# Layer 1's input weights asked for ahead of x, and the value's weights split ahead of the key's copy

## The chip, the cores and the metric

One core of one Trainium2 chip. The metric is the device time of one execution in microseconds (us), lower is better; before the change the median of three runs is 1089.43 us.

## The reference

Two layers of a diffusion backbone over 256 latent and 256 context tokens of 1024 features, float32. Each layer runs attention heads and a gated linear recurrence side by side on one input projection, then a mixture of 16 experts:

```python
def hybrid_layer(x, xc, mod, mod_c, p, router_w, router_b, cos, sin, last):
    ...
    h = modulate(rms_norm(x, p["norm1_g"]), sh1, sc1)
    hc = modulate(rms_norm(xc, p["norm1_g"]), csh1, csc1)
    mix, mix_c = parallel_mixers(h, hc, p, cos, sin, last)
    x = x + g1 * (mix @ p["w_out"])
    h2 = modulate(rms_norm(x, p["norm2_g"]), sh2, sc2)
    ...
    y = grouped_moe(tokens, *moe_w)
    x = x + g2 * y[:B * S].reshape(B, S, D)
```

`parallel_mixers` starts with `q, k, v, u, gb = jnp.split(h @ p["w_in"], cuts, axis=-1)`: the columns of `w_in` are query, key, value, the recurrence's input u and its gate. Layer 1 (the last) needs the context only for keys, values and the recurrence's start.

## The kernel before, in words

The stream x is `xtok`, four tiles of 128 tokens (tiles 0 and 1 context, 2 and 3 latent). In layer 0's experts (`experts`, L1476) each expert gathers its tokens, computes them on TensorE, and POOL adds its results to x in DRAM with a scattering DMA (`scatter`, L1493, into `yd`). x thus lies in DRAM when layer 0 ends. The experts have fixed slots; tokens beyond these are taken by an overflow block (L1759) that is skipped when there are none, as in these runs. Each engine that skips it raises its semaphore counts by what the block would have added: POOL does so for the eight counts of its own DMAs (DMASW0 to DMASW7), with one instruction.

Layer 1 begins in `mixer` (L478). `back_x` (L473) reloads x from `yd`, four DMAs of one tile each on SP's queue; `load_win` (L197) loads `w_in` in four pieces, the first `win_kv` (256 columns, key and value), the second u's 512 columns (`wu` in the code, tile `win`), then query and gate. After the first two come `load_adab` (small loads on POOL's queue) and `load_bd`. `norm1` (L404) then squares each tile of x on ScalarE (L412), forms the scale on VectorE, transposes and scales x on TensorE (`pxt`, with a diagonal matrix `dg`; nine warming products come ahead of it, on tile 1 of x), and shifts the result into `hT` (L427 on VectorE, L429 on ScalarE).

The key's projection (`proj`, `pproj<-hT,win_kv`) multiplies in full float32. All others (`proj3`) use split operands: a rounded part (fp32r) and the rest, three products with 24 matmuls. `piece` (L502) makes the two parts of four chunks of weights, a cast on ScalarE (L508) and a subtraction on VectorE (L509), into one of four slots of `wps`; h is split in the same way into `hh` (L867) and `hl` (L868). The value's two pieces are `pv_`; `k_squares` (L601 on) copies the key from PSUM and squares it, `k_sums` adds the squares up with a matmul (`pks`), for the key's norm.

In layer 1 the order of VectorE, POOL, ScalarE and SP is taken as the code writes it within a `manual_schedule` block, which ended after `norm1`; behind it, and for TensorE in all of this part, a scheduler sets the order.

Of the kernel before, what the change touches and what calls it, by code (L numbers as in the profile page):

```python
# [20 lines left out]
P = 128  # L21
# [91 lines left out]
def backbone(ctx: ExitStack, tc: tile.TileContext, a: dict):  # L113
    nc = tc.nc
    pe, act, dve, pool = nc.tensor, nc.scalar, nc.vector, nc.gpsimd

    def mm(out, lhsT, rhs, start, stop):
        pe.matmul(out, lhsT, rhs, start=start, stop=stop)  # L118
# [10 lines left out]
    def psb(name, tag, n=512):  # L129
        t = pp["pool"].tile([P, 512], F32, name=name, tag=tag, bufs=pp["bufs"][tag])  # L130
        return t[:, 0:n]

    def ps_mm(name, n=512):
        return psb(name, "mm", n)
# [28 lines left out]
    def C(n):  # L163
        o, w = COFF[n]
        return cst[:, o:o + w]
# [8 lines left out]
    def wchunk(name, pl=None, dt=F32):  # L174
        if pl is None:
            pl = wpool
        else:
            return pl.tile([P, 4096], dt, name=name, tag="w")
        if wx["pool"] is not None:
            if wx["only"] is None:  # L180
                i = wx["i"] % wx["n"]
                pl = wpool if i < 4 else wx["first"] if i < 4 + wx["nf"] else wx["pool"]
                wx["i"] += 1
            else:
                pl = wx["only"]
        return pl.tile([P, 4096], dt, name=name, tag="w")
# [10 lines left out]
    def load_win(l, lo, n, t=None):  # L197
        src = a["w_in"][l].rearrange("(k p) n -> p k n", p=P)
        t = (wchunk(f"win{l}_{lo}") if t is None else t)[:, 0:KC * n].rearrange("p (k n) -> p k n", k=KC)
        nc.sync.dma_start(t, src[:, :, lo:lo + n])  # L200
        return t

    WIN = ((512, 256), (768, 512), (0, 512), (1280, 512))
# [102 lines left out]
    def load_adab(l, tmp):  # L306
        for g in (1, 2, 3):
            b = adab[l, g] = tmp.tile([P, 512], F32, name=f"adab{g}", tag=f"adab{g}", bufs=1)
            pool.memset(b[:], 0.0)
            for r in range(2):  # L310
                if g < 3:
                    nc.gpsimd.dma_start(b[r::32, :], a["ada_b"][l, g * 2048:(g + 1) * 2048].rearrange("(j n) -> j n", j=4))
                else:
                    nc.gpsimd.dma_start(b[r:r + 64:32, :], a["norm2_g"][l].rearrange("(j n) -> j n", j=2))
# [158 lines left out]
    def back_x():  # L473

        for t in range(4):
            nc.sync.dma_start(xtok[:, t, :], tokens(yd[0])[t])

    def mixer(l, R, hp, hT, mo):  # L478
# [9 lines left out]
        order = ExitStack()  # L488
        if l:
            order.enter_context(tc.manual_schedule(engines={mybir.EngineType.DVE, mybir.EngineType.Pool, mybir.EngineType.Activation, mybir.EngineType.SP}))  # L490
        kv = tmp.tile([P, 2048], F32, name="win_kv", tag="rec", bufs=1)
        if l:
            back_x()
        win = [load_win(l, *WIN[0], kv), load_win(l, *WIN[1])]
        load_adab(l, tmp)
        if l == 0:
            load_consts()
# [4 lines left out]
        def piece(wv, on):  # L502

            wh, wl = wps[:, 0, wpi[0] % 4], wps[:, 1, wpi[0] % 4]
            wpi[0] += 1
            if len(wv.shape) == 3:
                wh, wl = (v.rearrange("p (k m) -> p k m", k=4) for v in (wh, wl))
            on(wh, wv)  # L508
            dve.tensor_tensor(wl, wv, wh.bitcast(F32), op=OP.subtract)  # L509
            return wh, wl  # L510

        def pieces(w, lo, on=act.copy):
            return [piece(w[:, k0:k0 + 4, lo:lo + P], on) for k0 in (0, 4)]

        if l == 0:
            pv_ = pieces(win[0], P)
        norm1(l, hT, tmp, lp, win[0])
        order.close()
        win += [load_win(l, *w) for w in WIN[2:]]
        if l:  # L520
            pv_ = pieces(win[0], P)
        hh, hl = lp.tile([P, KC, T], F32R, name="hh"), []


# [38 lines left out]
        wkv, wu, wq, wgb = win  # L563
# [7 lines left out]
        def proj3(ws):  # L571

            ps = ps_mm("pproj")
            for k0, (wh, wl) in zip((0, 4), ws):
                for i, (w, h) in enumerate(((wh, hh), (wl, hh), (wh, hl))):
                    for k in range(k0, k0 + 4):
                        mm(ps, w[:, k - k0, :], h[:, k, :] if h is hh else h[k // 2][:, k % 2, :], k + i == 0, k + i == KC + 1)
            return ps
# [22 lines left out]
        def k_squares(ps):  # L601
            act.copy(kT[:], ps)
            sq = t2("sqk")
            act.activation(sq[:], kT[:], AF.Square)
            return sq

        def k_sums(sq):
            pks = psb("pks", "sc")
            mm(pks, C("blk"), sq[:], True, True)
            return pks  # L610
# [252 lines left out]
        for k in range(KC):  # L863
            if k % 2 == 0:
                hl.append(hT_tile(l, F32R))
            x = hT[k // 2][:, k % 2, :]
            act.copy(hh[:, k, :], x)  # L867
            dve.tensor_tensor(hl[k // 2][:, k % 2, :], x, hh[:, k, :].bitcast(F32), op=OP.subtract)  # L868
        pu0 = pieces(wu, 0)
        sq = k_squares(ps)  # L870
        pv = proj3(pv_)
        pks = k_sums(sq)
        pu1 = pieces(wu, P)
        vc = t2("vc")
# [1145 lines left out]
    def layer(l, hp, hT, mo, ahead=None, after=None):  # L2020
        psum_pool(pst, f"pmx{l}", **MIX)
        last = l == DEPTH - 1
        lg, h2k = mixer(l, R, hp, hT, mo)
        pst.close()
        psum_pool(pst, f"pmo{l}", **MOE[l])
        tmp = mo.enter_context(tc.tile_pool(name=f"mo{l}", bufs=1, reuse_waits="tile"))
        if not last:
            blocks(l, tmp)
        with tc.tile_pool(name=f"rq{l}", bufs=1, reuse_waits="tile") as Q:
            route(l, lg, Q, R)  # L2030
        wx.update(pool=mo.enter_context(tc.tile_pool(name=f"wx{l}", bufs=NCH[l] - 4 - NF[l], side="right", reuse_waits="tile")), i=0, n=NCH[l], nf=NF[l], only=None)
        if last:
            experts_last(l, tmp, h2k[0], lambda: ahead(tmp), after)
        else:
            experts(l, tmp)
        pst.close()
        return tmp
# [3 lines left out]
    def hT_tile(l, dt):  # L2041
        return hps[l].tile([P, 2, T], dt, name=f"hT{l}", tag="hT", bufs=5)
# [98 lines left out]
```

## Time and profile before

| | us |
|---|---|
| median of three runs | 1089.43 (1086.31 to 1091.03) |
| the profiled execution | 1085.16 |
| its span, first to last instruction | 1083.4 |
| TensorE (PE) busy | 946.6 (87%) |
| VectorE (DVE) busy | 597.6 (55%) |
| ScalarE (ACT) busy | 436.6 (40%) |
| POOL busy | 186.0 (17%) |

The profile is of one execution. PE is TensorE's matmul row, PEld its weight loads, SPq the DMA issues of SyncE. "x8" is a count of merged instructions; a bracket at a row's end is the engine's idle time before it and what ended that. The granted clock of TensorE (PEclk) is 1.00 at 2.4 GHz and 0.50 at 1.2 GHz. Layer 0 ends and layer 1 begins near 607 us of the span.

### The profile page before, as it was taken

The numbers are of one execution on the slowest core, as the hardware profiler recorded it, in microseconds if no ns is written. First come the engines' busy times: TensorE is split into PE (matmuls) and PEld (weight loads), VectorE is DVE, ScalarE is ACT, GpSimd is POOL, SyncE is SP. The second block draws the span as 40 slices with busy tenths as digits, with TensorE's granted clock in tenths as the row PEclk, the third lists the DMA queues.
The fourth block names the chain that finished last, engine by engine and source line by source line (L and its number), as shares of the span: only waits on it lengthen the run. The fifth ranks groups of instructions, "written<-read, shape, count | busy, mean of one in ns | idle before, by whom it ended". The sixth has DMA issues, their size and how long they took to land. (4 is left out here: it accounts for less than half of the span.)

```text
span 1083.4 us, 16620 instructions
## 1 busy us (share of the span) xinstructions
PE 946.6 (87%) x6273; PEld 527.5 (49%) x6273; DVE 597.6 (55%) x1389; ACT 436.6 (40%) x871; POOL 186.0 (17%) x195
## 2 busy tenths in 40 slices
PE   6899999899879899998999599897997899768893
PEld 4565465577745444333333276343676445334431
DVE  3467587587752325544334456778867146344426
ACT  3636678465622212221221274886744223122212
POOL 2100023422352312221211300204332000000000
PEclk9999999899979999999999799997996899889886
DMA  9947675010739867999999484638229699999971
GB/s 374 409 165 286 226 294 215 30 39 28 295 141 379 268 256 260 389 415 410 394 396 386 142 309 161 232 131 335 74 74 386 228 426 424 421 427 419 425 328 42
DMA packets 58113, 299.00 MB, mean 276 GB/s; under 512 B 5456, under 2 KB 8400, under 8 KB 44160
## 3 DMA queue, kind: packets, MB, share of 16 engines
q1 hardware_dynamic: 50944, 279.88, 65.2%
q0 software_dynamic: 6896, 16.87, 5.5%
q8 instruction: 82, 1.34, 0.5%
q10 hardware_dynamic: 144, 0.52, 0.1%
q14 instruction: 47, 0.39, 0.1%
HBM read 288.86 MB, written 10.49 MB: 276 GB/s over the span
## 5 line engine op out<-in xcount | busy, mean ns | idle before, releaser
L118 PE MATMUL pgu<-wu,xgT 128*64 128x512 f32 x256 | 115.6, 602 | 0.5 <-SPq L1759 0.4
L118 PE MATMUL pgu<-wg,xgT 128*64 128x512 f32 x256 | 115.6, 602 | 0.3 <-ACT xgT L1505 0.3
L118 PE MATMUL pgu<-wu,xT 128*32 128x256 f32 (+1 forms) x416 | 88.7, 480 | 18.5 <-DMA wu<-exp_w_up_dram 18.5
L118 PE MATMUL pdn<-wd,hidT 128*64 128x512 f32 (+1 forms) x512 | 99.6, 598 | 1.8 <-PEq L1634 1.7
L118 PE MATMUL pgu<-wg,xT 128*32 128x256 f32 (+1 forms) x416 | 90.8, 482 | 6.4 <-DMA wg<-exp_w_gate_dram 4.1
L118 PE MATMUL pproj<-hh,wps 128*128 128x512 f32 x288 | 77.0, 407 | 0.0
L858 POOL TENSOR_TENSOR wo<-wf,wo 128x512 fp32r<-128x512 f32 x29 | 40.9, 1432 | 206.0 <-ACT wo L856 173.8
L1518 DVE TENSOR_TENSOR hid<-hid,pgu 64x512 f32<-64x512 f32 x16 | 11.0, 690 | 115.4 <-ACT hid L1517 115.3
L1493 POOL DMA_INDIRECT yd<-xtok,sgs x24 | 38.3, 1597 | 193.0 <-DVE xtok L1551 176.8
L1851 DVE TENSOR_TENSOR hid<-hid,pgu 64x512 f32<-64x512 f32 x16 | 11.0, 690 | 102.6 <-ACT hid L1850 102.6
L118 PEld LDWEIGHTS pgu<-wg,xgT 128*64 128x64 f32 x256 | 33.7, 138 | 65.2 <-issue 63.8
L118 PEld LDWEIGHTS pproj<-hh,wps 128*128 128x128 f32 x288 | 53.3, 188 | 19.5 <-issue 6.7
L118 PEld LDWEIGHTS pdn<-wd,hidT 128*64 128x64 f32 (+1 forms) x512 | 28.2, 128 | 55.3 <-issue 54.6
L118 PEld LDWEIGHTS pgu<-wu,xT 128*32 128x32 f32 (+1 forms) x416 | 33.4, 129 | 43.7 <-DMA wu<-exp_w_up_dram 23.2
L1517 ACT ACTIVATE hid<-pgu 64x512 f32<-64x512 f32 x16 | 9.4, 589 | 102.1 <-PE pgu L118 102.1
L1918 DVE SCALAR_TENSOR_TENSOR xtok<-pcb,wc,xtok 128x512 f32<-128x512 f32 x64 | 45.1, 747 | 9.0 <-PE pcb L118 7.4
L118 PEld LDWEIGHTS pgu<-wg,xT 128*32 128x32 f32 (+1 forms) x416 | 32.9, 129 | 30.5 <-issue 20.4
L1850 ACT ACTIVATE hid<-pgu 64x512 f32<-64x512 f32 x16 | 9.4, 590 | 91.6 <-PE pgu L118 91.6
L2070 POOL TENSOR_TENSOR fin<-xtok,fin 128x512 f32<-128x512 f32 x2 | 2.5, 1274 | 239.7 <-DVE xtok L1918 239.7
L807 ACT ACTIVATE Pm<-psc,mx,qy 128x512 f32<-128x512 f32 (+1 forms) x48 | 33.5, 702 | 20.9 <-DVE mx L801 20.8
L509 DVE TENSOR_TENSOR wps<-win,wps 128x512 fp32r<-128x512 f32 x48 | 32.7, 687 | 15.2 <-ACT wps L508 14.8
L118 PE MATMUL pproj<-hT,wps 128*128 128x512 f32 x144 | 39.8, 397 | 0.0
(457 smaller groups left out, 2119.4 us busy)
## 6 DMA issues: line engine op xcount, KB each, us to landing
wd<-exp_w_down_dram SPq DMA_DIRECT2D x31, 2048.0 KB
wu<-exp_w_up_dram SPq DMA_DIRECT2D x27, 2048.0 KB
wg<-exp_w_gate_dram SPq DMA_DIRECT2D x27, 2048.0 KB
xtok<-ada_w_dram SPq DMA_DIRECT2D x7, 2048.0 KB
win<-w_in_dram SPq DMA_DIRECT2D x6, 2048.0 KB
adac<-ada_w_dram SPq DMA_DIRECT2D x5, 2048.0 KB
xtok<-ada_w_dram SPq DMA_DIRECT2D x8, 1024.0 KB
adac<-ada_w_dram SPq DMA_DIRECT2D x8, 1024.0 KB
```

What stands on the lines that cost most here:

```text
L118: pe.matmul(out, lhsT, rhs, start=start, stop=stop)
L509: dve.tensor_tensor(wl, wv, wh.bitcast(F32), op=OP.subtract)
L807: act.activation(ps[h], sc_[i][h], AF.Exp, bias=mx[:, h:h + 1], scale=qr[:, ti, j, h:h + 1], accum_out=sm[:, h:h + 1])
L858: pool.tensor_tensor(lo, w, hi.bitcast(F32), op=OP.subtract)
L1493: st = pool.indirect_dma_start(out=dst, out_offset=bass.IndirectOffsetOnAxis(ap=idx, axis=0), in_=y, in_offset=None, bounds_check=dst.shap ...
L1517: mark.append(act.activation(sg, ps[0:64, :], AF.Silu).ins.name)
L1518: dve.tensor_tensor(h.rearrange("s k p -> s (k p)"), sg, ps[64:128, :], op=OP.mult)
L1850: act.activation(sg, ps[0:64, :], AF.Silu)
L1851: dve.tensor_tensor(h.rearrange("s k p -> s (k p)"), sg, ps[64:128, :], op=OP.mult)
L1918: dve.scalar_tensor_tensor(x, cb, wc[:, t, e:e + 1], x, op0=OP.mult, op1=OP.add)
L2070: (dve if q else pool).tensor_tensor(fin["t"][:, 1 + t, cs], x, fin["t"][:, 0, cs], op=OP.mult)
```

## The change

It does three things in `mixer`, for layer 1. The loads of `win_kv` and of u's weights are written ahead of `back_x`. The value's two pieces are no longer made after the fixed order's end, but inside the loop that splits h, after its chunks 3 and 5. And the fixed order (`order.close()`) ends later, behind the value's product. In layer 0 `win` is loaded where it was (there is no `back_x`), and its fixed order doesn't exist.

```diff
--- before.py
+++ after.py
@@ -489,9 +489,9 @@
         if l:
             order.enter_context(tc.manual_schedule(engines={mybir.EngineType.DVE, mybir.EngineType.Pool, mybir.EngineType.Activation, mybir.EngineType.SP}))
         kv = tmp.tile([P, 2048], F32, name="win_kv", tag="rec", bufs=1)
+        win = [load_win(l, *WIN[0], kv), load_win(l, *WIN[1])]
         if l:
             back_x()
-        win = [load_win(l, *WIN[0], kv), load_win(l, *WIN[1])]
         load_adab(l, tmp)
         if l == 0:
             load_consts()
@@ -515,10 +515,9 @@
         if l == 0:
             pv_ = pieces(win[0], P)
         norm1(l, hT, tmp, lp, win[0])
-        order.close()
         win += [load_win(l, *w) for w in WIN[2:]]
         if l:
-            pv_ = pieces(win[0], P)
+            pv_ = []
         hh, hl = lp.tile([P, KC, T], F32R, name="hh"), []
 
 
@@ -866,9 +865,12 @@
             x = hT[k // 2][:, k % 2, :]
             act.copy(hh[:, k, :], x)
             dve.tensor_tensor(hl[k // 2][:, k % 2, :], x, hh[:, k, :].bitcast(F32), op=OP.subtract)
+            if l and k in (3, 5):
+                pv_.append(piece(wkv[:, 4 * len(pv_):4 * len(pv_) + 4, P:2 * P], act.copy))
         pu0 = pieces(wu, 0)
         sq = k_squares(ps)
         pv = proj3(pv_)
+        order.close()
         pks = k_sums(sq)
         pu1 = pieces(wu, P)
         vc = t2("vc")
```

On SP, at the start of layer 1, with the counts that each issue waits for (DMASW: POOL's DMAs, DMAHW: SP's own), before:

```order
L476 DMA xtok<-yd_1344 128x1024 [waits DMASW4_49,DMASW3_49,DMASW6_49,DMASW2_49,DMASW7_49,DMASW1_49,DMAHW3_49,DMASW0_49,DVE_49]
L476 DMA xtok<-yd_1344 128x1024 [waits DMAHW4_49]
L476 DMA xtok<-yd_1344 128x1024 [waits DMAHW5_49,DMASW5_49]
L476 DMA xtok<-yd_1344 128x1024 [waits DMAHW6_49]
L200 DMA win_kv<-w_in_dram 128x8x256 [waits DMASW5_49,DMASW3_49,DMASW7_49,DMASW1_49,DMAHW7_49,PE_49,Pool_49]
L200 DMA win_768_9703<-w_in_dram 128x8x512 [waits DMAHW0_49]
L296 DMA bd<-lruw_dram 128x1024 [waits DMAHW1_49,Activation_49]
L200 DMA win_0_9846<-w_in_dram 128x8x512 [waits DMAHW2_49]
```

and now:

```order
L200 DMA win_kv<-w_in_dram 128x8x256 [waits DMASW3_49,DMASW5_49,DMASW2_49,DMASW6_49,DMASW1_49,DMASW7_49,DMASW0_49,DMAHW3_49,PE_49,Pool_49]
L200 DMA win_768_9699<-w_in_dram 128x8x512 [waits DMAHW4_49]
L476 DMA xtok<-yd_1344 128x1024 [waits DMASW4_49,DMASW6_49,DMASW2_49,DMAHW5_49,DMASW0_49,DVE_49]
L476 DMA xtok<-yd_1344 128x1024 [waits DMAHW6_49]
L476 DMA xtok<-yd_1344 128x1024 [waits DMAHW7_49]
L476 DMA xtok<-yd_1344 128x1024 [waits DMAHW0_49]
L296 DMA bd<-lruw_dram 128x1024 [waits DMAHW1_49,Activation_49]
L200 DMA win_0_9845<-w_in_dram 128x8x512 [waits DMAHW2_49]
```

The two loads of w_in stand ahead of the four of x. win_kv, which waited for four of POOL's counts, waits for seven, and the first x tile for four instead of seven; bd and what follows stand where they stood.

On POOL, the end of layer 0 in the changed kernel (the last scatters of the experts, then the test at L1761 for the overflow block, and the ISA instruction that raises the eight counts where it is skipped; the same rows stand in the kernel before, at L1759):

```order
L1495 DMA yd_1344<-xtok,sgs 2048x256 [waits DVE_49]
L1636 COMPARE_AND_BRANCH
L1636 ISA [waits DMASW4_49]
L1636 UNCONDITIONAL_BRANCH
L1495 DMA yd_1344<-xtok,sgs 2048x256 [waits DVE_49]
L1636 UNCONDITIONAL_BRANCH
L1760 TENSOR_LOAD oi [waits DVE_49]
L1761 COMPARE_AND_BRANCH
L1761 ISA [waits Pool_sequencer_49,DMASW4_49,DMASW5_49,DMASW3_49,DMASW6_49,DMASW2_49,DMASW7_49,DMASW1_49,DMASW0_49]
L1761 UNCONDITIONAL_BRANCH
```

Nothing moved here; the last ISA waits for all eight counts first.

On ScalarE, from the end of the shifts to the key's copy and square (hT are the shifted tiles, hh their rounded parts, wps the rounded weights, kT the key), before:

```order
L429 ACTIVATE hT_9684<-pxt,mod_135,A_1_137 128x256
L867 CAST hh<-hT_9683 128x512
L429 ACTIVATE hT_9685<-pxt,mod_135,A_1_137 128x256
L867 CAST hh<-hT_9683 128x512
L867 CAST hh<-hT_9684 128x512 x2
L867 CAST hh<-hT_9685 128x512 x2
L602 COPY kT<-pproj 128x512
L604 ACTIVATE sqk<-kT 128x512
L508 CAST wps<-win_kv 128x512 x2
L508 CAST wps<-win_768_9703 128x512 x4
```

and now:

```order
L429 ACTIVATE hT_9685<-pxt,mod_135,A_1_137 128x256
L866 CAST hh<-hT_9682 128x512 x2
L866 CAST hh<-hT_9683 128x512 x2
L508 CAST wps<-win_kv 128x512
L866 CAST hh<-hT_9684 128x512 x2
L508 CAST wps<-win_kv 128x512
L866 CAST hh<-hT_9685 128x512 x2
L508 CAST wps<-win_768_9699 128x512 x2
L601 COPY kT<-pproj 128x512
L603 ACTIVATE sqk<-kT 128x512
L508 CAST wps<-win_768_9699 128x512 x2
```

The casts of win_kv moved from behind the key's square to among the casts of hh, the first two of u's weights to just ahead of the key's copy, and the casts of hh no longer alternate with the shifts. VectorE's subtractions follow the same order.

On TensorE the scheduler has moved pks, one product, from ahead of the value's 24 matmuls to behind them; on POOL the two memsets of the convolution's edges (`up`) stand behind the small loads of `adab` instead of ahead of them.

## Rows read from the trace of the kernel before

**Rows 1.** TensorE's timeline between the layers.

```profile
603.21 3.65 PE L118 MATMUL pdn<-wd,hidT 128*64 128x512 f32 x16
619.29 4.02 PE L118 MATMUL warm<-ident,xtok 128*128 128x128 f32 x18 [12.43 <-DMA xtok<-yd]
623.15 7.42 PE L118 MATMUL pxt<-dg,xtok 128*128 128x128 f32 x64
630.41 7.03 PE L118 MATMUL pproj<-hT,win_kv 128*128 128x512 f32 x16
638.78 1.13 PE L118 MATMUL pks<-sqk,cst 128*128 128x512 f32 x2 [1.34 <-ACT sqk L604]
639.34 2.42 PE L118 MATMUL pproj<-hh,wps 128*128 128x512 f32 x8
```

**Rows 2.** Busy time by stretch: length, PE, PEld, DVE, ACT, POOL, PEclk, DMA share, GB/s.

```profile
607.00:619.00 12.00, 0.00 (x0) 0.00 (x0) 2.00 (x5) 1.15 (x2) 3.72 (x7) 0.60 0.52 133
614.10:616.00 1.90, 0.00 (x0) 0.00 (x0) 0.00 (x0) 0.00 (x0) 0.00 (x0) 0.50 0.46 140
614.10:619.20 5.10, 0.00 (x0) 0.00 (x0) 0.15 (x1) 1.17 (x3) 2.37 (x6) 0.50 0.80 261
614.10:622.90 8.80, 3.61 (x17) 3.64 (x18) 2.65 (x19) 3.49 (x7) 5.14 (x11) 0.50 0.89 307
616.00:624.00 8.00, 4.71 (x26) 4.74 (x27) 2.65 (x19) 4.59 (x8) 5.14 (x11) 0.56 1.02 356
624.00:632.00 8.00, 8.00 (x62) 7.13 (x62) 5.65 (x23) 7.74 (x18) 0.00 (x0) 1.00 1.06 402
```

**Rows 3.** POOL's timeline at the end of layer 0, and the last scatter's landing.

```profile
608.72 1.55 POOL L1493 DMA_INDIRECT yd<-xtok,sgs  x1 [4.10 <-DVE xtok L1551]
...
DMA to landing us min/median/max: 4.8/4.8/4.8
```

**Rows 4.** SP's timeline, its DMA issues from layer 0's last on.

```profile
586.34 0.38 SPq L220 DMA_DIRECT2D wd<-exp_w_down_dram  x1
614.10 1.78 SPq L476 DMA_DIRECT2D xtok<-yd  x4
616.11 0.39 SPq L200 DMA_DIRECT2D win_kv<-w_in_dram  x1
616.55 0.62 SPq L200 DMA_DIRECT2D win<-w_in_dram  x1
617.27 5.83 SPq L296 DMA_DIRECT2D bd<-lruw_dram  x1
```

**Rows 5.** ScalarE's timeline, the squares of x's tiles 0, 1 and 3.

```profile
617.43 1.06 ACT L412 ACTIVATE sq<-xtok 128x1024 bf16<-128x1024 f32 x1 [13.79 <-DMA xtok<-yd]
...
619.18 1.06 ACT L412 ACTIVATE sq<-xtok 128x1024 bf16<-128x1024 f32 x1 [0.60 <-DMA xtok<-yd]
...
622.86 1.06 ACT L412 ACTIVATE sq<-xtok 128x1024 bf16<-128x1024 f32 x1 [0.19 <-DMA xtok<-yd]
```

**Rows 6.** ScalarE's timeline behind the key's projection.

```profile
637.48 0.59 ACT L602 COPY kT<-pproj 128x512 f32<-128x512 f32 x1 [3.33 <-PE pproj L118]
...
638.63 1.12 ACT L508 CAST wps<-win_kv 128x512 fp32r<-128x512 f32 x2
```

**Rows 7.** DMA issues of the whole execution, with the size of one.

```profile
win<-w_in_dram SPq DMA_DIRECT2D x6, 2048.0 KB
...
win_kv<-w_in_dram SPq DMA_DIRECT2D x2, 1024.0 KB
...
xtok<-yd SPq DMA_DIRECT2D x4, 512.0 KB
```

**Rows 8.** Start of the program: SP's issue of win_kv, TensorE's waits for ada_w and it.

```profile
6.99 0.38 SPq L200 DMA_DIRECT2D win_kv<-w_in_dram  x1
...
30.24 1.06 PE L118 MATMUL pada<-ada,csil 128*32 128x512 f32 x8 [1.47 <-DMA ada<-ada_w_dram]
...
33.20 3.32 PE L118 MATMUL warm<-ident,win_kv 128*128 128x128 f32 x16 [0.16 <-DMA win_kv<-w_in_dram]
```

**Rows 9.** TensorE's longest waits from 640 us to the end: us, times, longest.

```profile
PE pgu L118 <- DMA wu<-exp_w_up_dram: 18.5, 6, 4.2
...
PE psc L118 <- ACT Pm L807: 3.0, 1, 3.0
```

## The prediction, before the result was known

> **What bounds the kernel now.** I read the busy time by stretch first, then the timelines of the queues and engines between the layers. TensorE sets the pace nearly everywhere, and the reader should look for the place where it stands still: from the end of layer 0's last down product (603.21 + 3.65 = 606.86 us) to the first warming product at 619.29 it does nothing, 12.43 us, and the row names the load of x as what ended that [rows 1]. In 607 to 619 us its busy time is 0.00 and DMA moves 133 GB/s; from 616 on DMA is full, at 356 and then 402 GB/s [rows 2]. So this stretch first waits, then queues.
>
> What it waits for is a chain of one piece after the other. POOL's last scatter into yd is issued at 608.72 and lands 4.8 us later, at 613.5 [rows 3]; SP issues the four reloads of x from 614.10, then win_kv at 616.11 and the next input weights at 616.55 [rows 4]. The squares on ScalarE start at 617.43 (tile 0), 619.18 (tile 1) and 622.86 (tile 3), each ended by its x tile [rows 5]. The transposes (64 passes, two for each float32 product) start at 623.15, run without a gap, and hand over to the key's projection at 630.41 [rows 1]. No row has TensorE waiting for w_in here: in layer 1 the weights come early enough although they are asked for last. After the key, TensorE waits once more: 1.34 us before pks [rows 1], because ScalarE copies the key (637.48), squares it and only then splits the value's weights (638.63) [rows 6].
>
> **Part 1: w_in ahead of x.** Nothing is added or removed; two DMAs, 1024 and 2048 KB, pass four of 512 KB [rows 7], that is 3.146 MB ahead of 2.097 MB. What decides is when SP may issue them. Before, x waits for counts of POOL's DMAs, and the scatter's is among them. In the new order win_kv waits for seven such counts, PE and POOL. In the program as built, four of the seven (DMASW1, 3, 5, 7) must reach values that they get only from the step of 64 that POOL adds to all eight counts when it skips the overflow block (L1759), and POOL adds it after it has waited for all eight, the last scatter's included. So win_kv is released with x, not before it: I expect its issue at 614.1. Upper bound: these four counts are seen satisfied only by win_kv's own issue at 616.11 [rows 4], 2.0 us later; I take 0, since x needs the other four from the same step and goes at 614.10.
>
> Then x lies behind 3.146 MB. That a later load on SP's queue lands after an earlier one, the start of the program shows: win_kv is issued at 6.99, TensorE gets the last of the ada_w loads issued ahead of it at 30.24, and win_kv itself only at 33.20 [rows 8]. The Trainium skill ("DMA: Bandwidth & Descriptors", section "Queues, rings and completion order") says that each DMA engine takes its descriptors in ring order, though completion need not keep that order; this speaks against the change, and rows 8 agree with it.
>
> The price is 3.146 MB at the rate of the stretch. By 356 GB/s [rows 2] it is 8.8 us, by win_kv's own 2.96 us for 1.049 MB at the start [rows 8] 8.9, by 420 (above the 402 of rows 2, the upper end) 7.5. I follow the curve of rows 2. Tile 1 landed when 5.1 us x 261 GB/s = 1.33 MB had moved; it now needs 4.48 MB. By 616 0.27 MB had moved (1.9 us x 140), by 624 0.27 + 8 us x 356 = 3.12 MB, and the other 1.36 MB at 402 take 3.4 us: 627.4, **8.2 us later** [rows 2]. Tile 3: 8.8 us x 307 = 2.70 MB, now 5.85 MB: 630.8, 7.9 us later; its scaling is then ready with the first half of the transposes, as now, so tile 1 decides. That sum over a page's figure: the same page ("Anatomy of one DMA") fits 436 GB/s to the moving part, which by itself would make it 7.2 us and the sum 1.0 us smaller; the 356 and 402 GB/s of rows 2 are measured here and decide.
>
> What lies behind x on SP (bd at 617.27, blocked in its issue for 5.83 us, then two more w_in, ada_w) [rows 4] has the same bytes ahead of it as before and doesn't land later; none of it is waited for in this stretch. POOL's two memsets of the convolution's edges move behind its small loads: not wanted before the convolution, nothing. The granted clock is at 0.50 in 614 to 622.9 already [rows 2], so a longer stop can't lower it as shown; the warming products start with tile 1 as now and move along: nothing.
>
> **Part 2: the value's weights split ahead of the key's copy.** Two casts (ScalarE) and two subtractions (VectorE) move forward among the splits of h, which both engines do while the key's projection runs, 630.41 to 637.44 [rows 1]. ScalarE's eight casts of h and four of weights at some 0.6 us (1.12 for two [rows 6]) follow the last shift near 631 and end near 637.6, about where the key's copy starts now. The value's product can follow the key's at once, and pks (which only moves behind it) no longer stalls: **-1.3 us** (the 1.34 of rows 1). Bounds: 0, if the casts are not ready; -1.9, the 637.44 to 639.34 between the two products with pks [rows 1], if pks too hid elsewhere. I take 1.3 because pks still has to run.
>
> **Sum.** +8.2 - 1.3 = +6.9 us. Does a later stage swallow it? From the value on, TensorE's waits are short and for other engines, and the large ones, 18.5 us for wu, are in layer 1's experts [rows 9], whose loads go out as chunks come free behind TensorE: they move along. The profiled execution is 1085.16 us, so 1092.1 by it; the median of the three runs is 4.3 us above it, 1089.43, and by that I forecast **1096.3 us**. From the bounds 7.5 - 1.9 and 8.9 + 2.0 - 0: 1095.0 to 1100.3. About 0.5%, 5.4 us, is what a measurement of this kernel can tell from no change: 1084.0 to 1094.9.
>
> **Rivals.**
> - The weights leave early (the other side: not slower). If win_kv's wait is met before the scatter lands, w_in moves while SP and DMA idle (SP issues nothing from 586.34 to 614.10 [rows 4]). It decides if w_in is out 3.146 / 0.4 = 7.9 us ahead, by 606. x is then not delayed, and it lands without sharing: tile 3 came after 2.70 MB though x is 2.10, 0.6 MB or 1.6 us. With part 2: -2.9, 1086.5. Against: POOL's step comes after the scatter. The Trainium skill's same page ("Rules for kernel authors") advises to issue a DMA early and wait late; by that rule this is the case that holds, and no row of this trace shows it between the layers. Chance 0.15.
> - The loads share the engines instead of queueing: x gets half the rate while w_in runs, and is late by half of 8.2 less the 1.3: +2.8, 1092.2. For: the 0.6 MB of others' bytes that overtook x [rows 2]. Against: rows 8. Chance 0.15.
> - It costs more: release at 616.1, or x's issue blocked behind 2048 rows of weights as bd was for 5.83 us [rows 4]: up to 2 more, 1098.3. For: bd. Against: the weights' own issues, 0.39 and 0.62 us. Chance 0.10.
>
> **Numbers.** The forecast has 0.60: slower 0.52, within 0.5% 0.07 (three runs spread over 4.7 us), faster 0.01. Early weights: 0.10 within, 0.05 faster. Sharing: 0.13 within, 0.02 slower. Costing more: 0.10 slower. Together slower 0.64, within 0.30, faster 0.06. The range reaches down past the sharing case, into runs of an unchanged kernel, and up to the dearer one: 1088.5 to 1100.
>
> **What would show it.** Right: win_kv's issue at 614.1, x's from about 615; TensorE's idle time before the warming products some 20.6 instead of 12.43 us; transposes at 631.3; no wait between key and value; everything after about 7 us later. Wrong: a DMA of w_in before 613, x's squares within 3 us of their present times, or a wait of 1 us or more left behind the key.

## The result, and the profile after

The changed kernel takes 1092.22 us (median of 21 runs) where the kernel before takes 1085.56 (21 runs beside them): 6.7 us slower, a ratio of 1.0062 with a 95% interval of 1.0046 to 1.0079 (5.0 to 8.6 us). One run of the changed kernel, 1148.13 us at a granted clock of 0.813 instead of 0.93, is left out of the ratio. The forecast was +6.9 us. Its absolute figure, 1096.3, is 4 us high because it stood on a median of three runs, 1089.43, and more runs put the kernel before at 1085.56. The profiled execution of the changed kernel took 1090.43 us, its span is 1088.7.

SP's timeline, the DMA issues of the changed kernel from layer 0's last on (compare [rows 4]):

```profile
585.03 0.38 SPq L220 DMA_DIRECT2D wd<-exp_w_down_dram  x1
613.01 0.40 SPq L200 DMA_DIRECT2D win_kv<-w_in_dram  x1
613.47 0.57 SPq L200 DMA_DIRECT2D win<-w_in_dram  x1
614.28 2.80 SPq L476 DMA_DIRECT2D xtok<-yd  x4
617.18 0.87 SPq L296 DMA_DIRECT2D bd<-lruw_dram  x1
```

POOL's last scatter (compare [rows 3]) and ScalarE's squares of x's tiles 0, 1 and 3 (compare [rows 5]):

```profile
607.37 1.55 POOL L1495 DMA_INDIRECT yd<-xtok,sgs  x1 [4.07 <-DVE xtok L1553]
```

```profile
625.56 1.06 ACT L412 ACTIVATE sq<-xtok 128x1024 bf16<-128x1024 f32 x1 [23.24 <-DMA xtok<-yd]
...
626.78 1.06 ACT L412 ACTIVATE sq<-xtok 128x1024 bf16<-128x1024 f32 x1
...
629.40 1.06 ACT L412 ACTIVATE sq<-xtok 128x1024 bf16<-128x1024 f32 x1 [0.19 <-DMA xtok<-yd]
```

win_kv goes out 5.64 us after the scatter's issue; before, x went 5.38 us after it. Nothing of w_in left early. Tile 0 of x now lands 18.2 us after the scatter's issue instead of 8.7 (617.43 - 608.72), with tile 1 right behind it.

TensorE's timeline of the changed kernel between the layers (compare [rows 1]):

```profile
601.90 3.65 PE L118 MATMUL pdn<-wd,hidT 128*64 128x512 f32 x16
626.90 4.18 PE L118 MATMUL warm<-ident,xtok 128*128 128x128 f32 x18 [21.34 <-DVE n1m L371]
630.87 7.67 PE L118 MATMUL pxt<-dg,xtok 128*128 128x128 f32 x64
638.37 7.03 PE L118 MATMUL pproj<-hT,win_kv 128*128 128x512 f32 x16
644.84 2.42 PE L118 MATMUL pproj<-hh,wps 128*128 128x512 f32 x8
...
650.83 1.02 PE L118 MATMUL pks<-sqk,cst 128*128 128x512 f32 x2
```

The stop ahead of the warming products grew from 12.43 to 21.34 us. What the row names as its end is `n1m`, the first step of the scale of x's tiles 0 and 1 on VectorE, and not the load of x as before; tile 1 landed just ahead of it (see the price, below). The value's product follows the key's without a wait, and pks stands behind it. The reason is on ScalarE, whose casts of win_kv now come ahead of the key's copy (compare [rows 6]):

```profile
641.11 0.62 ACT L508 CAST wps<-win_kv 128x512 fp32r<-128x512 f32 x1
...
642.67 0.61 ACT L508 CAST wps<-win_kv 128x512 fp32r<-128x512 f32 x1
...
645.44 0.59 ACT L601 COPY kT<-pproj 128x512 f32<-128x512 f32 x1
```

Busy time by stretch, columns as in [rows 2]:

```profile
607.00:619.00 12.00, 0.00 (x0) 0.00 (x0) 0.53 (x2) 0.00 (x0) 4.47 (x7) 0.53 0.59 158
613.00:616.00 3.00, 0.00 (x0) 0.00 (x0) 0.00 (x0) 0.00 (x0) 0.51 (x1) 0.50 0.57 147
616.00:624.00 8.00, 0.00 (x0) 0.00 (x0) 0.00 (x0) 0.00 (x0) 4.70 (x11) 0.50 1.06 400
624.00:632.00 8.00, 5.10 (x25) 5.13 (x26) 4.04 (x31) 4.60 (x8) 0.00 (x0) 0.52 1.03 407
613.00:625.50 12.50, 0.00 (x0) 0.00 (x0) 0.00 (x0) 0.00 (x0) 5.21 (x11) 0.50 0.94 339
613.00:626.10 13.10, 0.00 (x0) 0.00 (x0) 0.00 (x0) 0.54 (x1) 5.21 (x11) 0.50 0.94 343
```

TensorE does nothing while w_in streams in, and from 616 us on DMA is full. From win_kv's issue until tile 0 is there, 12.5 us x 339 GB/s = 4.24 MB have moved, w_in's 3.146 and 1.09 more.

Layer 0 ends at another time in each execution (in the profiles of the table the last scatter is issued between 607.4 and 613.3 us), so times between the layers are best read from that scatter's issue. The start of each step less that issue, us, each from the timeline of its kernel's profile; "w_in ahead" is what stands ahead of x on x's queue and is released with it, "ada" is the first product with ada_w, behind the value and the first product of u:

| kernel | w_in ahead, MB | warming | transposes | key | value | ada |
|---|---|---|---|---|---|---|
| before | 0 | 10.57 | 14.43 | 21.69 | 30.62 | 42.30 |
| the change | 3.146 | 19.53 | 23.50 | 31.00 | 37.47 | 50.00 |
| loads_only | 3.146 | 19.47 | 23.45 | 31.48 | 37.95 | 50.48 |
| gap_kept | 3.146 | 18.96 | 22.90 | 30.04 | 38.97 | 50.67 |
| split_only | 0 | 10.46 | 14.43 | 22.59 | 29.06 | 41.59 |
| split_free | 0 | 10.43 | 14.40 | 22.31 | 31.25 | 42.93 |
| kv_ahead | 1.049 | 13.92 | 17.89 | 25.69 | 32.16 | 44.71 |
| q_ahead | 5.243 | 24.31 | 27.92 | 35.07 | 41.53 | 54.06 |
| other_queue | 0 (3.146 beside) | 12.12 | 16.09 | 23.53 | 30.00 | 42.53 |
| u_early_l1 | 0 | 10.45 | 14.27 | 21.79 | 28.26 | 40.79 |
| u_after_silu | 0 | 12.80 | 16.76 | 23.90 | 30.37 | 42.91 |

Each row is one execution. How long the transposes take varies with when the granted clock rises: from 7.1 us (gap_kept, u_after_silu) to 8.2 us (split_only) from their start to the key. What follows ada, up to the last instruction, takes 426.4 us (loads_only) to 432.4 us (before), without following the order of the rows. Differences of 1 us at ada, and of several at the end, are therefore read from medians and not from one profile.

### The profile page after: what moved, and what is told of

Its sections match the earlier page's. It is cut to its first block, busy times and chain, and to the rows that moved or that the text cites. A ratio compares the mean times of both kernels' runs of the same rounds, so it can differ in the third digit from the quotient of the medians.

```text
span 1088.7 us, 16615 instructions
## 1 busy us (share of the span) xinstructions
PE 945.8 (87%) x6273; PEld 526.5 (48%) x6273; DVE 598.9 (55%) x1389; ACT 436.1 (40%) x871; POOL 186.0 (17%) x195
```

## The experiments

Eleven kernels ran, in three rounds; the kernel before ran beside each round, at 1085.58, 1087.17 and 1085.80 us. Ratios are to those runs.

### What is each part worth?

**loads_only**, the first part alone:

```diff
         kv = tmp.tile([P, 2048], F32, name="win_kv", tag="rec", bufs=1)
+        win = [load_win(l, *WIN[0], kv), load_win(l, *WIN[1])]
         if l:
             back_x()
-        win = [load_win(l, *WIN[0], kv), load_win(l, *WIN[1])]
```

> The loads of win_kv and u's weights ahead of x, the value's split and the fixed order's end as before. Queue theory (x waits behind 3.146 MB, the split gives back the wait between key and value): all of the delay and none of the gain. In the profile of the change the transposes came 9.0 us later after layer 0's last product and 1.6 us were back by the first ada product behind the value, so about 8 us over the kernel before (its median 1085.6): 1093 to 1095; TensorE idle 21 us ahead of the warming products, and a wait of 1.3 us for sqk behind the key. Rival 'the split gives nothing': the same time as the change, 1092.2. Rival 'the cost lies in the split or the fixed order': no slower than before, 1085.6.

Measured: 1091.66 us, ratio 1.0065 (1.0041 to 1.0090), the same as the change. That is under the 1093 to 1095 expected, and what the rival 'the split gives nothing' said. The idle time is as expected, the gap is not. TensorE's and ScalarE's timelines of this kernel:

```profile
631.13 4.18 PE L118 MATMUL warm<-ident,xtok 128*128 128x128 f32 x18 [21.31 <-DMA xtok<-yd]
...
643.14 7.03 PE L118 MATMUL pproj<-hT,win_kv 128*128 128x512 f32 x16
649.61 2.42 PE L118 MATMUL pproj<-hh,wps 128*128 128x512 f32 x8
```

```profile
642.30 0.61 ACT L508 CAST wps<-win_kv 128x512 fp32r<-128x512 f32 x1
...
650.21 0.59 ACT L602 COPY kT<-pproj 128x512 f32<-128x512 f32 x1 [1.18 <-PE pproj L118]
```

There is no wait between key and value here either. With w_in written ahead of x, the scheduler, which sets the order behind the norm in this kernel, places the casts of win_kv among the last shifts by itself, and pks behind the value. The second part of the change is therefore worth nothing that can be measured on top of the first.

**gap_kept**, the change with the old order of the splits forced, to see the loads' price without that:

```diff
-            if l and k in (3, 5):
-                pv_.append(piece(wkv[:, 4 * len(pv_):4 * len(pv_) + 4, P:2 * P], act.copy))
-        pu0 = pieces(wu, 0)
+        if not l:
+            pu0 = pieces(wu, 0)
         sq = k_squares(ps)
+        if l:
+            pv_ = pieces(wkv, P)
+            pu0 = pieces(wu, 0)
```

> The change with w_in ahead of x, but the value's and u's weights split behind the key's copy in the fixed order, as the kernel before had them. In loads_only the scheduler itself had put the casts ahead of the key's copy, so the gap was gone there and the loads' whole price was not seen alone. Theory: the gap of 1.3 us or more before pks is back and the time is 1.5 us over the change, 1093.5 to 1094 (8 us over before). Rival 'the gap is worth nothing behind a late x': 1092.2.

Measured: 1094.68 us, ratio 1.0080 (1.0048 to 1.0112), 2.5 us over the change and 8.9 over the kernel before. The two ratios' intervals overlap, so the times alone do not show the gap's worth. The gap is back, and TensorE's timeline says for what:

```profile
641.05 7.03 PE L118 MATMUL pproj<-hT,win_kv 128*128 128x512 f32 x16
649.42 1.12 PE L118 MATMUL pks<-sqk,cst 128*128 128x512 f32 x2 [1.34 <-ACT sqk L603]
```

In the table the stretch from the key to ada is 20.63 us here and 20.61 before; in the change and in loads_only it is 19.00. By this stretch the gap is worth 1.6 us.

**split_only**, the second part alone, with `back_x()` ahead of the loads as before and the rest as changed.

> The value's split and the longer fixed order alone, x asked for first as before. Queue theory: the loads' whole cost is gone and the gap's gain stays, 1.3 to 1.9 us under before: 1083.7 to 1084.3; TensorE idle 12.4 us ahead of the warming products, no wait between key and value. Rival 'the wait only moves' (a later wait for the weights or the small sums takes it back): 1085.6, same as before. Rival 'the split costs' (casts delay the shifts or the key's copy): over 1086.5.

Measured: 1084.05 us, ratio 0.9980 (0.9961 to 0.9999), 1.5 us under the kernel before. TensorE's timeline:

```profile
620.17 4.18 PE L118 MATMUL warm<-ident,xtok 128*128 128x128 f32 x18 [12.52 <-DVE n1m L371]
624.14 8.32 PE L118 MATMUL pxt<-dg,xtok 128*128 128x128 f32 x64
632.30 7.03 PE L118 MATMUL pproj<-hT,win_kv 128*128 128x512 f32 x16
638.77 2.42 PE L118 MATMUL pproj<-hh,wps 128*128 128x512 f32 x8
```

The loads' whole cost is gone and the gain stays: this is the part of the change to keep. The interval only just leaves out no change, and u_after_silu, below, is as fast. Its profile shows the 1.56 us at the value (29.06 against 30.62), but only 0.7 at ada, because its transposes ran slower here: the granted clock was still 0.50 in their first 2 us, so the key starts 0.9 us later than before. What the medians give, 1.5 us, is the better figure.

**split_free**, as split_only, but with the fixed order ending behind the norm, as before:

```diff
         norm1(l, hT, tmp, lp, win[0])
+        order.close()
...
         pv = proj3(pv_)
-        order.close()
```

> The value's split in the loop, x first, the fixed order ending behind the norm as before. Theory 'the place of the casts is all': as split_only, 1084.0, no wait between key and value. Rival 'the longer fixed order does it': the scheduler puts the casts where it likes and the gap of 1.3 us is back, 1085.6.

Measured: 1087.04 us, ratio 0.9996 (0.9973 to 1.0019). By its interval this time alone can't be told from split_only's, but TensorE's timeline shows the old wait, and the rival holds:

```profile
642.39 1.12 PE L118 MATMUL pks<-sqk,cst 128*128 128x512 f32 x2 [1.34 <-ACT sqk L604]
```

Writing the split into the loop does nothing while the scheduler may move it back behind the key's square. Of the change's second part, the later `order.close()` is what makes it hold. It is not enough by itself: gap_kept has the later end too, with the splits written behind the key's copy, and there the wait is as long.

### What does x pay for?

**kv_ahead** and **q_ahead**: fewer bytes and more bytes ahead of x. The first:

```diff
-        win = [load_win(l, *WIN[0], kv), load_win(l, *WIN[1])]
+        win = [load_win(l, *WIN[0], kv)]
         if l:
             back_x()
+        win.append(load_win(l, *WIN[1]))
```

> The change with only win_kv (1.049 MB) ahead of x, u's weights behind it. Queue theory, a price by bytes: a third of the change's 9.0 us, 3.0, less the split's 1.6: 1.4 us over before, 1087.0; TensorE idle 15.3 us ahead of the warming products. Rival 'a fixed price' (the first load ahead of x costs by its release or its issue, whatever its size): as the change, 1092, idle 21 us. Rival 'shared rate' (x moves beside w_in at half rate): idle 13.9 us, 1085.5.

The second asks for the query's weights ahead of x too (the lines not shown set up `wps` ahead of that load as well):

```diff
         win = [load_win(l, *WIN[0], kv), load_win(l, *WIN[1])]
...
         if l:
...
+            win.append(load_win(l, *WIN[2]))
             back_x()
...
-        win += [load_win(l, *w) for w in WIN[2:]]
+        win += [load_win(l, *w) for w in WIN[len(win):]]
```

> The change with a third load, the query's weights (2.097 MB more, 5.243 MB in all), ahead of x. Queue theory: by the slope of the change, 9.0 us for 3.146 MB, another 5.2 to 6.0 us (2.097 MB at 402 to 350 GB/s): TensorE idle 26.5 to 27.5 us ahead of the warming products, 1097.5 to 1098.5. Rival 'shared rate': x shares only as long as it moves, so a third load that starts later adds little: idle 21 to 23 us, 1092 to 1094.

Measured: kv_ahead 1088.16 us, ratio 1.0010 (0.9985 to 1.0036); q_ahead 1096.48 us, ratio 1.0096 (1.0068 to 1.0123). TensorE's timelines of the two:

```profile
627.24 4.18 PE L118 MATMUL warm<-ident,xtok 128*128 128x128 f32 x18 [15.68 <-DMA xtok<-yd]
```

```profile
634.21 3.77 PE L118 MATMUL warm<-ident,xtok 128*128 128x128 f32 x18 [25.95 <-DMA xtok<-yd]
```

The idle times are near the queue theory's 15.3 and 26.5 to 27.5 us, and far from the rivals' 21 and 21 to 23; q_ahead is 0.6 us of idle time and 1.0 us of time under what I expected. The price goes by bytes. Over the kernels with the split, from 0 to 1.049, 3.146 and 5.243 MB, the warming starts at 10.46, 13.92, 19.53 and 24.31 us: 3.3, 2.7 and 2.3 us for each further MB, or 303, 374 and 439 GB/s. The medians, 1084.05, 1088.16, 1092.22 and 1096.48, rise with them by 4.1, 4.1 and 4.3 us; the first step is large for its bytes, but kv_ahead's interval is 5.5 us wide. A price that does not depend on size is out, and so is x sharing the engines with what stands ahead of it on its queue: the third load would then have added little.

**other_queue**: the same two loads issued by ScalarE instead of SP.

```diff
-        nc.sync.dma_start(t, src[:, :, lo:lo + n])
+        q.dma_start(t, src[:, :, lo:lo + n])
...
+        wq_ = nc.scalar if l else nc.sync
+        win = [load_win(l, *WIN[0], kv, q=wq_), load_win(l, *WIN[1], q=wq_)]
```

> The change with the two loads of w_in issued by ScalarE, on its own queue, and x by SP, both released by POOL's step. Queue theory (the order within one queue makes x wait): x shares the engines with w_in and is later than before but earlier than in the change; half rate for its 2.1 MB gives some 4 us less than the change's 9: TensorE idle 15 to 18 us, 1086.5 to 1089.5. Rival 'the engines, not the queue' (what is asked for first is moved first, or both load at the sum's rate until both are done): as the change, idle 21 us, 1092. Rival 'x is not touched by another queue': idle 12.5 us, 1084.

Measured: 1088.13 us, ratio 1.0006 (0.9977 to 1.0034). ScalarE's and SP's issues and TensorE's warming:

```profile
618.86 0.42 ACTq L200 DMA_DIRECT2D win_kv<-w_in_dram  x1
619.48 0.44 ACTq L200 DMA_DIRECT2D win<-w_in_dram  x1
```

```profile
618.78 2.25 SPq L476 DMA_DIRECT2D xtok<-yd  x4
```

```profile
625.46 4.18 PE L118 MATMUL warm<-ident,xtok 128*128 128x128 f32 x18 [13.71 <-DMA xtok<-yd]
```

The two queues are released within 0.1 us of each other (618.86 and 618.78) and the same bytes are asked for, but the warming is 1.6 us later than before instead of 9.0 (table). I had expected 15 to 18 us of idle time; 13.71 is under that. How the queues share shows in their packets, MB and share of the engines' time from x's issue to the warming (618.7 to 625.5 us; q1 is SP's queue, q10 ScalarE's):

```profile
q1 hardware_dynamic: 361, 1.35, 55.1%
q10 hardware_dynamic: 716, 0.73, 31.0%
```

When tile 1 of x was in, SP's queue had moved 1.35 MB, as it had in the kernel before (1.33 by the prediction's sum), and only 0.73 MB of w_in went beside it. At the 370 and 403 GB/s that this kernel moved in 621 to 623 and 623 to 625 us, 0.73 MB is 1.8 to 2.0 us, an estimate near the 1.6. So most of x's price in the change is its place on one queue; the load on the engines costs it what w_in moves meanwhile. The Trainium skill ("DMA: Bandwidth & Descriptors", section "Queues, rings and completion order") says that a DMA engine takes one ring's descriptors in order and goes round between the rings of different queues packet by packet; these two runs agree, 9.0 us on one queue and 1.6 on two, and the 1.35 and 0.73 MB show that both queues moved at once, though not with equal bytes.

### Can w_in leave early?

**u_early**: only u's weights ahead of x. Their buffer is one of four weight chunks that the overflow block doesn't use.

```diff
-        win = [load_win(l, *WIN[0], kv), load_win(l, *WIN[1])]
+        wu_ = load_win(l, *WIN[1])
         if l:
             back_x()
+        win = [load_win(l, *WIN[0], kv), wu_]
```

> With the value's split. u's weights (2.097 MB) are asked for ahead of x, win_kv behind it. u's buffer is one of the four weight chunks, which the overflow block doesn't use, so its issue waits for one of SP's own earlier loads alone and stands ahead of the test for the overflow block; only win_kv's buffer waits for POOL's raised counts. Theory 'the buffer's wait sets the price': u leaves at about 588, 25 us ahead of x, and x pays nothing: TensorE idle at most 12.5 us ahead of the warming products, down to 10.9 if u was among what overtook x; 1082.4 to 1084.1. Rival 'whatever stands ahead of x on its queue costs its bytes': 2.097 MB at some 380 GB/s, 5.5 us more idle, 1089.5. Rival 'it is paid in layer 0' (u's load delays the last down weights): TensorE's wait for wd behind 588 grows, time 1085 or more.

Measured: 1093.03 us, ratio 1.0052 (1.0030 to 1.0075). The load did leave early, as SP's timeline shows, and TensorE's shows what it met:

```profile
593.77 0.38 SPq L220 DMA_DIRECT2D wd<-exp_w_down_dram  x1
594.99 0.38 SPq L200 DMA_DIRECT2D win<-w_in_dram  x1
624.49 2.23 SPq L476 DMA_DIRECT2D xtok<-yd  x4
```

```profile
609.89 1.08 PE L118 MATMUL pdn<-wd,hidT 128*64 128x512 f32 x4 [1.62 <-issue]
...
612.50 5.25 PE L118 MATMUL pdn<-wd,hidT 128*64 128x512 f32 x16
```

So u's own buffer does not tie it to the scatter: its weights went 1.22 us behind the last wd and 29.5 us ahead of x. In the change they stand behind win_kv on SP, and it is win_kv's buffer that waits for POOL's counts. But the edit had a flaw: it swapped the two loads in layer 0 too, whose end came later (wd's last issue at 593.77, in the other profiles 585.0 to 591.1), and layer 0's last down products stalled, 5.25 us instead of 3.65. The last scatter came 25.06 us after the last wd's issue instead of 22.38, and the warming 12.56 us after the scatter instead of 10.57. 'It is paid in layer 0' thus holds for a good part; why x, too, came later isn't shown.

**u_early_l1**: the same for layer 1 only.

> As u_early, but layer 0 keeps its order of the first loads (u_early also put u's load ahead of win_kv there, and its layer 0 ended some 8 us later). Theory 'u_early's time was paid in layer 0': its last scatter came 25.1 us after the last wd's issue instead of 22.2 to 22.6, so 2.6 us stay there, 1.2 us are left ahead of the warming products (13.65 instead of 12.4), and the split gives 1.5: 1085.6 + 2.6 + 1.2 - 1.5 = 1087.9. Rival 'a load 25 us ahead of x costs its bytes all the same': 1090 or more. Rival 'all of the loss was the order in layer 0': 1084.

Measured: 1087.17 us, ratio 1.0009 (0.9990 to 1.0027). Of u_early's 5.9 us over the kernel before, 4.5 went with layer 0's old order. In the profile x pays nothing (10.45 in the table), and the last scatter comes 22.82 us after the last wd's issue, 22.38 before, with 0.93 us of waiting for issue among layer 0's last products. I had expected 1087.9, which is near, but of its two losses, 2.6 and 1.2 us, the profile shows 0.4 and none: that the number fits is luck. The time should then be near split_only's, yet it is not under the kernel before's. Its interval, 1.1 us under to 2.9 over, leaves room for chance, and this stays open.

**u_after_silu** and **u_after_weigh**: u's load also waits for a point of the last expert, its silu on ScalarE or its last result on VectorE (`after=` adds that wait to the load):

```diff
+        wu_ = load_win(l, *WIN[1], after=wx["mark"]) if l else None
...
+        win = [load_win(l, *WIN[0], kv), wu_ or load_win(l, *WIN[1])]
```

> As u_early_l1, but u's load also waits for the last expert's silu on ScalarE, some 12 us after the last wd's issue, when wd is in and DMA moves only 50 to 110 GB/s; x is asked for some 15 us later. Theory 'early is free in an idle stretch': no delay in layer 0 (last scatter 22.4 us after the last wd's issue), TensorE idle 11 to 12.5 us ahead of the warming products: 1082.5 to 1084.1, the best of all. Rival 'it still stalls the last expert' (fetches of instructions behind u's descriptors): last scatter 24 us or more after wd's issue, 1086 to 1087.

> As u_early_l1, but u's load also waits for layer 0's last result on VectorE, together with the last scatter, 5.5 us ahead of x's issue. Theory 'price by the bytes still ahead when x is asked for': u's 2.1 MB begin to move some 2 us after their issue, so about 1.3 MB are in by x's issue and 0.8 MB, 2 us, lie ahead of it; TensorE idle 13.5 to 14.5 us, 1085.6 + 1.5 - 1.5 = 1085 to 1086. Rival 'the scatter is held up too' (u moves while the last scatter does): x's issue later than 5.8 us after the scatter, 1087 or more.

Measured: u_after_silu 1084.22 us, ratio 0.9987 (0.9962 to 1.0011), the same as split_only without any early load; the warming came 12.80 us after the scatter, 2.3 later than in split_only, the last scatter 23.34 us after the last wd's issue, and TensorE stalled 1.13 us for issue in layer 0's last products. The time is in the range expected, but the stretch is not: TensorE's idle time is 13.87 us, over the 11 to 12.5, and what x waited for isn't shown. An early load in an idle stretch is not dear, but nothing is won by it. u_after_weigh 1092.52 us, ratio 1.0069 (1.0038 to 1.0100), as slow as the change and not the 1085 to 1086 expected; its rival 'the scatter is held up too' holds. Its profile is of the fastest of its seven runs, 1086.54. SP's timeline and SP's waits (waited for: us, times, longest) of u_after_weigh:

```profile
608.25 0.38 SPq L220 DMA_DIRECT2D win<-w_in_dram  x1
621.88 1.77 SPq L476 DMA_DIRECT2D xtok<-yd  x4
```

```profile
SPq L220 <- DVEq L1762: 21.3, 1, 21.3
SPq L1762 <- SPq L1762: 9.6, 1, 9.6
```

u's load was issued 0.46 us behind the last scatter (607.79). SP then waited 9.6 us at L1762, where it skips the overflow block and first waits for all of its own DMAs, u's load among them, which landed 10.4 us after its issue, at 618.65. POOL's scatter landed after 9.8 us instead of 4.8:

```profile
DMA to landing us min/median/max: 9.8/9.8/9.8
```

x went out 14.1 us after the scatter, not 5.4. Both waits end near 618 us, but SP's is the one that held x last. In the kernel before x went 0.6 us behind the scatter's landing, here 4.3 us behind it (621.88 against 617.6), while POOL's next work came as soon after the landing as before, 3.2 us (620.77) and 3.0. What SP did in the 3.2 us between u's landing and x's issue no row shows.

## Why the prediction was right

**The release: right.** I expected w_in to be released with x, at 614.1, because of POOL's raised counts. It went 5.64 us after the scatter, in the other kernels with w_in first 5.4 to 5.7, and x before at 5.38. The upper bound of 2.0 us wasn't needed. u_early shows the other side: a load whose buffer doesn't wait for those counts, and that stands behind none that does, is gone 29.5 us ahead of x.

**The price, 8.2 us: right in kind, 0.8 too small.** The warming came 8.96 us later. From the release the forecast had it at 13.4 us (5.2 before and 8.2 more); it came at 13.9 (626.90 - 613.01), and the release itself was 0.26 us later against the scatter. The time for the bytes was right, the bytes were not. The 4.48 MB of the forecast had moved by 626.1 us (13.1 us x 343 GB/s), 0.3 us sooner than the sum said. But tile 1 was not in then. The times from issue to landing, of tile 0 (issued at 614.28) and of tiles 0 and 1 together (tile 1 issued at 615.71), give its landing:

```profile
xtok<-yd SPq DMA_DIRECT2D x1, 512.0 KB, 11.2
...
xtok<-yd SPq DMA_DIRECT2D x2, 512.0 KB, 11.1
```

With 11.2 us for tile 0 and 11.1 in the middle of the two, tile 1 took some 11.0 us: it landed near 626.7, with about 4.7 MB moved. So about 0.25 MB more of others' bytes than in the kernel before went ahead of it, 0.6 us, and n1m came 0.2 us behind. "Tile 1 decides" is thus nearly right: in this execution tile 0's sum, through n1m, came as late. The rates that I took from [rows 2], 356 and 402 GB/s, became 400 and 407, and the first 3 us behind the release moved 147 GB/s. That a later load on the queue waits for an earlier one rested on rows from the program's start; kv_ahead, q_ahead and other_queue now show it here, and they agree with the rule of the Trainium skill's page that spoke against the change. The 436 GB/s of the same page ("Anatomy of one DMA") is fitted there to DMAs that POOL issues, and these are SP's. It is not reached in any stretch shown (q_ahead's 439 is a difference of two executions), and its 7.2 us were further from the 8.96 than the 8.2 of the rows.

**The granted clock at no cost: nearly.** The transposes took 7.67 us instead of 7.42, because the granted clock was still at its lower level, 0.50, when they began, and rose within their first microsecond. In the kernel before it was 1.00 from their start. Their first microsecond in the change and in split_only:

```profile
630.87:631.87 1.00, 1.00 (x7) 1.00 (x7) 1.00 (x8) 0.00 (x0) 0.00 (x0) 0.63 1.05 410
```

```profile
624.14:625.14 1.00, 1.00 (x6) 1.00 (x6) 0.29 (x4) 0.68 (x2) 0.02 (x1) 0.50 1.10 367
```

So the clock cost 0.25 us here, which the forecast put at nothing. It is no price of a longer stop: split_only, with a stop as before, took 8.32 us, and q_ahead, with the longest, 25.95 us, took 7.31.

**The gap, 1.3 us: nearly right in size, wrong in whose it is.** From the key to ada the change saves 1.61 us (20.61 - 19.00). The sum is right because it counts the gap once. But the step gave it to part 2, and loads_only shows that part 1 closes the gap by itself, as the scheduler answers to the new order of the loads. Part 2 gains only where part 1 isn't: split_only, 1.5 us.

**The sum and what follows.** At ada the change is 7.7 us behind (50.00 - 42.30). At the end, scatter to last instruction, it is 481.3 to 474.7, 6.6 us, and the medians say 6.7. One pair of profiles can't show that "they move along": loads_only is 8.2 us behind at ada and 2.2 at the end. The medians carry it, to within their 5.0 to 8.6 us. That 6.9 met 6.7 so closely is in part luck: the price was 0.8 too small, the gap 0.3, the transposes cost 0.25, and 1.1 us that nothing forecast was gone at the end.

**The rivals.** "The weights leave early" fails by the release; where u's load alone leaves early, it gives no more than the split does (1084.22 and 1084.05), so the 1.6 us that I gave it for an x without company weren't seen; win_kv stood behind x in that kernel, and no kernel had both loads early. "The loads share the engines" is what other_queue does, and there x costs less than the 4.1 us I took for half rate: 1.6. "It costs more" fails: x's four issues took 2.80 us instead of 1.78, but they were done at 617.1, 8.4 us before tile 0 landed.

## What to carry to other kernels

A load that the next stage waits for goes first on its queue: each MB put ahead of it cost 2.3 to 3.3 us here, and asking early buys nothing when the buffer, not the issue's place, sets the release. Look at what the early load's buffer waits for before moving it, and if it must move along with the urgent one, give it another queue (1.6 us here instead of 9.0). When an edit moves loads, compare the order that the scheduler then gives the engines too, since a gain credited to one part may come with the other.

## What was not expected

A load of 2.1 MB beside layer 0's last expert was not free although TensorE's own weights had been asked for ahead of it: its last products stalled 1.62 us for issue in u_early, 0.93 in u_early_l1 and 1.13 in u_after_silu, and in none of the profiles without an early load. That the load is the cause is likely by this, but how isn't shown. And a skipped block isn't free of waits: SP stood 9.6 us at the test in u_after_weigh, for a load that the block doesn't use. In the kernel before it waits at the test too, 14.0 us in three waits, but these are over before x is wanted.
